# Gate and up projections of four feed-forward layers by seven block products in place of eight

## The chip, the core and the metric

One core of a Trainium2 chip runs the whole program. The metric is the device time of one execution in microseconds (us). The kernel before takes 2497.47 us (median of three runs, 2493.9 to 2501.86).

Engines are named as in the profile: PE (matrix products; PEld is its loading of the stationary operand), DVE (vector engine), ACT (activation engine), POOL (general engine), SP (a queue that issues transfers). Each engine works through its own list in order; semaphores tie the lists together.

## The reference

A sequence of 512 positions with 1024 features goes through four layers. Each adds a mixer's output to the stream and then a feed-forward block. Only this block matters here; it occurs four times (2816 hidden columns each):

```python
def swiglu(h, w_in, w_out):
    gu = h @ w_in
    gate, up = gu[..., :D_FF], gu[..., D_FF:]
    return (jax.nn.silu(gate) * up) @ w_out

x = x + swiglu(rmsnorm(x, norm_ffn_w[i]), ffn_w_in[i], ffn_w_out[i])
```

`rmsnorm` multiplies each position (a row of `h`) by one factor, 1/sqrt(mean of squares + eps), and each feature by a weight. Everything is float32.

## The kernel before

The stream lies transposed in eight tiles `xT[k]` of 128 features x 512 positions. Each float32 operand is split into a rounded part and a rest, `hi` and `lo`, both in the rounded type fp32r, and one product becomes three matmuls: hi*hi, hi*lo, lo*hi (`mm3`, L203 to L206).

**Weights.** `load_raw` (L173) fetches 512 KB (four 128-row tiles x 256 columns) into one of three buffers `wraw`. `split` (L166) makes `whi` on ACT (L169) and `wlo` on DVE, in some mixers on POOL (L164), 512 elements per partition at a time, two splits per transfer; there are seven `whi` and seven `wlo` buffers.

**Norm.** `norm` (L253) multiplies each `xT[k]` by the feature weight into `xh`, `xl` (L276, L277), squares on ACT, adds the squares on POOL (L269), and then makes the row factor: `xs.rc` (one column per 128 positions) and `xs.rb` (the same, broadcast over partitions). The row factor is applied to the products afterwards.

**Feed-forward.** `pair(jj)` (L356) works out 256 gate columns and 256 up columns: four output blocks of 128 x 512, each 8 feature tiles x 3 matmuls of 512 columns, so 96 matmuls; there are 11 pairs per layer. `evac` (L345) multiplies the gate block by the row factor (DVE L347), applies silu (ACT L349), multiplies by the row factor again (POOL L350) and by the up block (DVE L351), and splits the result into `hhi`, `hlo` (L220, L221). After pairs 0 to 3, 4 to 7 and 8 to 10 `out_part` (L369) multiplies by the output weights and adds into `xT` (L394); in the last layer `out_nat` (L395) does it in the layout of the output, with 128 x 512 blocks that end in square, row factor and store (L433 to L448).

**What sets the order.** The program text only says what depends on what. A list scheduler with a timeline model fixes the order of each engine's list when the program is built; buffers are handed out in rotation, and an instruction that writes a buffer waits until the previous user of it is done. The eight accumulation banks (128 x 512 float32) are shared in a feed-forward block as g 2, s 3, t 2, o 1 (`PB[4]`, L89).

Of the kernel before, what the change touches and what calls it, by code (L numbers as in the profile page):

```python
# [16 lines left out]
P = 128  # L17
# [40 lines left out]
def tile_net(ctx: ExitStack, tc: tile.TileContext, d, out, layers=(0, 1, 2, 3)):  # L58
# [33 lines left out]
    hidden = [None]  # L92
# [11 lines left out]
    WB = 7  # L104
# [61 lines left out]
    def split(raw, nk, n):  # L166
# [172 lines left out]
    def ffn(L, last=False, aside=None):  # L339
        wi, wd = f"in{L}", f"down{L}"  # L340
        xs = norm(f"ffn{L}")
        parts = [(0, 8), (8, 16), (16, 22)]
        hid = {}

        def evac(j, pg, pu):  # L345
            g = scr("fg")
            V.tensor_tensor(g, pg, xs.rb, op=ALU.mult)  # L347
            s = scr("fs")
            A.activation(s, g, AF.Silu)  # L349
            G.tensor_tensor(s, s, xs.rb, op=ALU.mult)  # L350
# [4 lines left out]

        def pair(jj):  # L356
            bg = load_a(wi, 0, KT, jj * 256, 256)
            bu = load_a(wi, 0, KT, DFF + jj * 256, 256)
            if jj == 0:
                pss = group_a(xs, [bg[0], bu[0], bg[1], bu[1]], ["g", "g", "s", "s"])  # L360
                evac(0, pss[0], pss[1])
                evac(1, pss[2], pss[3])
            else:
                for i in range(2):
                    pg = group_a(xs, [bg[i]], ["g"])[0]
                    pu = group_a(xs, [bu[i]], ["g"])[0]
                    evac(2 * jj + i, pg, pu)

        def out_part(p):  # L369
            a, b = parts[p]  # L370
# [5 lines left out]
            for g in range(4):  # L376
                blocks = load_a(wd, a, n, g * 256, 256)
                if p == 2 and g < 2:
# [8 lines left out]
                    for m, ps in enumerate(pss):  # L387
                        V.tensor_tensor(xT[m], ps, xT[m], op=ALU.add)
                    continue
                for i, b in enumerate(blocks):  # L390
# [3 lines left out]
                    V.tensor_tensor(xT[m], ps, xT[m], op=ALU.add)  # L394
# [1202 lines left out]
```

## Time and profile before

| | us |
|---|---|
| median of three runs | 2497.47 |
| profiled execution, its own time | 2493.01 |
| span of the profile | 2491.3 |
| PE busy | 2437.0 (98%) |
| DVE busy | 1419.6 (57%) |
| ACT busy | 998.0 (40%) |
| POOL busy | 526.7 (21%) |

The profiled execution's time is 1.7 us above its span. Busy time of PE is modelled: a matmul's shown duration runs past the start of the next one, so pace is read from the distance of starts, and idle time from the list of waits.

### The profile page before, as it was taken

The page shows a single profiled execution, that of the slowest core. Times are in us where ns is not written, and L with a number is a line of the kernel's source. Part 1 is how long each engine was busy: PE and PEld are TensorE (multiplying, and loading weights), DVE is VectorE, ACT ScalarE, POOL GpSimd, SP SyncE. Part 2 cuts the span into 40 slices and gives each one's busy share as a digit, 9 for nine tenths or more (in the row PEclk, how much of TensorE's full clock was granted, in tenths as well). Part 3 has the DMA queues.
Part 4 walks back from the last instruction along what each step waited for, and adds up shares of the span by engine and source line. Part 5 has one row for each costly group of instructions (what it writes and reads, how often), then busy time and mean ns, then how long its engine had stood idle before and what let it go on. Part 6 is the DMA issues. An engine that isn't in the chain of part 4 may idle for free. (4 is left out here: it accounts for less than half of the span.)

```text
span 2491.3 us, 30631 instructions
## 1 busy us (share of the span) xinstructions
PE 2437.0 (98%) x11316; PEld 1990.8 (80%) x11316; DVE 1419.6 (57%) x2613; ACT 998.0 (40%) x1900; POOL 526.7 (21%) x429
## 2 busy tenths in 40 slices
PE   8999999999999999999999988999999999999998
PEld 7897888888767888888767866888888888888887
DVE  6577644445786643435889978743434755434335
ACT  4444423334586432323554463432323323323333
POOL 3220101002362200101656345310101201100000
PEclk9999999999999999999999999999999999999999
DMA  4332333322311332332221133233332333223332
GB/s 138 115 100 69 94 102 94 100 91 89 106 39 35 93 101 94 100 95 86 73 78 60 52 108 96 92 95 101 93 101 78 110 102 102 94 89 104 96 96 74
DMA packets 73559, 226.26 MB, mean 91 GB/s; under 512 B 10353, under 2 KB 14593, under 8 KB 73409
## 3 DMA queue, kind: packets, MB, share of 16 engines
q1 hardware_dynamic: 68896, 220.00, 28.9%
q10 hardware_dynamic: 4464, 4.21, 0.6%
q8 instruction: 89, 1.46, 0.2%
q14 instruction: 62, 0.50, 0.1%
q0 software_dynamic: 48, 0.10, 0.0%
HBM read 219.45 MB, written 2.20 MB: 89 GB/s over the span
## 5 line engine op out<-in xcount | busy, mean ns | idle before, releaser
L169 ACT ACTIVATE whi<-wraw 128x512 fp32r<-128x512 f32 (+1 forms) x798 | 492.7, 622 | 1062.5 <-PE ps_g L205 702.8
L164 DVE TENSOR_TENSOR wlo<-wraw,whi 128x512 fp32r<-128x512 f32 (+1 forms) x738 | 540.8, 736 | 462.1 <-ACT whi L169 440.2
L204 PE MATMUL ps_g<-xh,whi 128*128 128x512 f32 x1976 | 780.8, 395 | 6.0 <-DVE fg L347 1.9
L205 PE MATMUL ps_g<-xl,whi 128*128 128x512 f32 x1976 | 776.1, 393 | 0.5 <-POOL xl L221 0.5
L206 PE MATMUL ps_g<-xh,wlo 128*128 128x512 f32 x1976 | 774.2, 392 | 0.0
L204 PEld LDWEIGHTS ps_g<-xh,whi 128*128 128x128 f32 x1976 | 372.9, 189 | 87.4 <-issue 4.3
L206 PEld LDWEIGHTS ps_g<-xh,wlo 128*128 128x128 f32 x1976 | 372.5, 188 | 79.3 <-issue 1.7
L205 PEld LDWEIGHTS ps_g<-xl,whi 128*128 128x128 f32 x1976 | 373.0, 189 | 77.6 <-issue 0.9
L350 POOL TENSOR_TENSOR fs<-fs,rb 128x512 f32<-128x512 f32 x88 | 114.5, 1302 | 1160.0 <-ACT fs L349 1160.0
L347 DVE TENSOR_TENSOR fg<-ps_g,rb 128x512 f32<-128x512 f32 x84 | 58.0, 691 | 142.9 <-PE ps_g L206 142.9
L351 DVE TENSOR_TENSOR fg<-ps_g,fs 128x512 f32<-128x512 f32 x84 | 58.0, 691 | 129.5 <-PE ps_g L206 128.0
L269 POOL TENSOR_TENSOR ssum<-ssum,sq 128x512 f32<-128x512 f32 x56 | 79.6, 1422 | 163.8 <-ACT sq L268 162.3
L164 POOL TENSOR_TENSOR wlo<-wraw,whi 128x512 fp32r<-128x512 f32 (+1 forms) x60 | 80.0, 1340 | 107.5 <-ACT whi L169 97.2
L204 PE MATMUL ps_s<-hhi,whi 128*128 128x512 f32 x264 | 102.7, 389 | 0.0
L205 PE MATMUL ps_s<-hlo,whi 128*128 128x512 f32 x264 | 102.7, 389 | 0.0
L206 PE MATMUL ps_s<-hhi,wlo 128*128 128x512 f32 x264 | 102.7, 389 | 0.0
L204 PE MATMUL ps_t<-hhi,whi 128*128 128x512 f32 x264 | 102.7, 389 | 0.0
L205 PE MATMUL ps_t<-hlo,whi 128*128 128x512 f32 x264 | 102.7, 389 | 0.0
L206 PE MATMUL ps_t<-hhi,wlo 128*128 128x512 f32 x264 | 102.7, 389 | 0.0
L220 ACT ACTIVATE hhi<-fg 128x512 fp32r<-128x512 f32 x88 | 55.6, 632 | 32.8 <-DVE fg L351 32.6
L277 DVE SCALAR_TENSOR_TENSOR xl<-xT,cols,xh 128x512 fp32r<-128x512 f32 x64 | 63.8, 1007 | 8.0 <-ACT xh L276 8.0
L349 ACT ACTIVATE fs<-fg 128x512 f32<-128x512 f32 x88 | 55.6, 632 | 30.8 <-DVE fg L347 30.8
(494 smaller groups left out, 3611.4 us busy)
## 6 DMA issues: line engine op xcount, KB each, us to landing
wraw<-in_in_dram SPq DMA_DIRECT2D x176, 512.0 KB, 3.5
wraw<-in_down_dram SPq DMA_DIRECT2D x82, 512.0 KB, 3.6
wraw<-in_par_in_dram SPq DMA_DIRECT2D x30, 512.0 KB, 3.5
wraw<-in_mlstm_in_dram SPq DMA_DIRECT2D x24, 512.0 KB, 4.0
wraw<-in_sc_in_dram SPq DMA_DIRECT2D x24, 512.0 KB, 3.7
wraw<-in_attn_in_dram SPq DMA_DIRECT2D x12, 512.0 KB, 3.8
wraw<-in_par_out_dram SPq DMA_DIRECT2D x12, 512.0 KB, 3.5
mb<-drs SPq DMA_DIRECT2D x16, 256.0 KB, 3.9
```

Of the source, the lines that this page charges most:

```text
L164: (V if e == "V" else G).tensor_tensor(lo, x, hi.bitcast(F32), op=ALU.subtract)
L169: A.activation(hi, raw, AF.Copy)
L204: T.matmul(o, lhsT=w[0], rhs=x[0], start=start, stop=False)
L205: T.matmul(o, lhsT=w[0], rhs=x[1], start=False, stop=False)
L206: T.matmul(o, lhsT=w[1], rhs=x[0], start=False, stop=stop)
L220: A.activation(hi, src, AF.Copy)
L269: G.tensor_tensor(ssum, ssum, sq, op=ALU.add)
L277: V.scalar_tensor_tensor(lo, xT[k], col(wname, k), hi.bitcast(F32), op0=ALU.mult, op1=ALU.subtract)
L347: V.tensor_tensor(g, pg, xs.rb, op=ALU.mult)
L349: A.activation(s, g, AF.Silu)
L350: G.tensor_tensor(s, s, xs.rb, op=ALU.mult)
L351: V.tensor_tensor(g, pu, s, op=ALU.mult)
```

## The change

The 1024 x 512 weight block of one pair (256 gate and 256 up columns) and the 1024 x 512 activations are each seen as a 2 x 2 matrix of blocks: weights by even and odd feature tile and by gate and up, activations by even and odd feature tile and by first and second half of the positions. The 2 x 2 product takes seven block products in place of eight, with sums of blocks ahead of and behind them (Winograd's form of Strassen's scheme).

- The four sums of activation blocks (`T1` to `T4`) are made once per layer (`combine`: two ACT scalings, three DVE subtractions, one split per pair of feature tiles).
- The weights of each pair are summed anew (`weights`): one addition on POOL (line 400 of the new kernel) and three subtractions on DVE (line 405), each 128 x 1024. Each of the seven operands is split 1024 wide (ACT line 170, DVE line 165).
- Each block product is 2 x 4 x 3 = 24 matmuls of 256 columns (lines 421 to 423) into one bank; products accumulate onto earlier ones in three of seven cases. ACT copies four intermediate sums out (`keep`, line 430), DVE adds them to later ones (lines 442, 448, 453, 455).
- Pair 0 of each layer is computed as before (96 matmuls of 512 columns), with banks s, o, s, o.
- The second row factor is taken off the hidden tile (the POOL multiplication is gone) and put on the output: `add_row` multiplies the output block by `xs.rb` (line 493) and then adds (line 494); in the last layer one instruction does both.
- Buffers: `wraw` five in place of three; `whi` and `wlo` four of 1024 in place of seven of 512, in the mixers too. The last layer's output runs in four parts (3, 3, 3, 2 pairs) in place of three. The rope tables use other buffers. The rows of the input weights are packed even tiles first.

```diff
-    WB = 7
+    WB = 4
+    RB = 5
...
-        return [(hi[:, k, :], lo[:, k, :]) for k in range(nk)]
+        return hi, lo
...
+            hi, lo = split(raw, m, n)
             for b in range(0, n, P):
-                res[b // P] += split(raw[:, :, b:b + P], m, P)
+                res[b // P] += [(hi[:, i, b:b + P], lo[:, i, b:b + P]) for i in range(m)]
...
-        parts = [(0, 8), (8, 16), (16, 22)]
+        parts = [(0, 3), (3, 6), (6, 9), (9, 11)] if last else [(0, 4), (4, 8), (8, 11)]
         hid = {}
...
+        rb2 = bass.AP(tensor=xs.rb.tensor, offset=xs.rb.offset, ap=[xs.rb.ap[0], [0, 2], [1, S]])
+        HS = slice(0, S // 2), slice(S // 2, S)
+        def gate(g):
+            V.tensor_tensor(g, g, rb2, op=ALU.mult)
+            A.activation(g, g, AF.Silu)
+        def store(jj, u):
+            n = 3 if last else 4
+            hi = hidden[0].tile([P, 2, S], F32R, tag="hhi", name="hhi", bufs=n)
+            lo = hidden[0].tile([P, 2, S], F32R, tag="hlo", name="hlo", bufs=n)
+            hilo(u, hi, lo)
+            for i in range(2):
+                hid[2 * jj + i] = (hi[:, i, :], lo[:, i, :])
+        tc_hi, tc_lo = [], []
+        def combine(i):
+            y = scr("S", (P, 2, S), bufs=3)
+            for h in range(2):
+                A.activation(y[:, h, :], xT[2 * i + h], AF.Copy, scale=col(f"ffn{L}", 2 * i + h))
+            t = scr("fu", (P, 4, S // 2))
+            hs = [y.ap[0], [S // 2, 2], [1, S // 2]]
+            V.tensor_tensor(t[:, 0:2, :], y[:, :, HS[1]], bass.AP(tensor=y.tensor, offset=y.offset, ap=hs),
+                            op=ALU.subtract)
+            V.tensor_tensor(t[:, 2, :], y[:, 1, HS[1]], t[:, 0, :], op=ALU.subtract)
+            V.tensor_tensor(t[:, 3, :], y[:, 1, HS[0]], t[:, 2, :], op=ALU.subtract)
+            hi = hidden[1].tile([P, 4, S // 2], F32R, tag="thi", name="thi", bufs=4)
+            lo = hidden[1].tile([P, 4, S // 2], F32R, tag="tlo", name="tlo", bufs=4)
+            hilo(t, hi, lo)
+            tc_hi.append(hi)
+            tc_lo.append(lo)
+        def quad(q):
+            if q[0] == "B":
+                k, h = int(q[1]) - 1, HS[int(q[2]) - 1]
+                return [(hi[:, h], lo[:, h]) for hi, lo in xs.t[k::2]]
+            n = ("T1", "T3", "T2", "T4").index(q)
+            return [(hi[:, n, :], lo[:, n, :]) for hi, lo in zip(tc_hi, tc_lo)]
+        STEPS = ("B11", "B21", "T1", "T2", "B22", "T3", "T4")
+        live = {}
+        def weights(jj, s):
+            if s == 0:
+                for n, (k, c) in enumerate(((0, 0), (4, 0), (0, DFF), (4, DFF))):
+                    live[jj, n] = load_raw(wi, k, c + jj * 256)
+                live[jj, "S1"] = scr("S", (P, 4, 256), bufs=3)
+                G.tensor_tensor(live[jj, "S1"], live[jj, 2], live[jj, 3], op=ALU.add)
+            r = [live[jj, n] for n in range(4)]
+            if s in (3, 4, 5):
+                t = scr("S", (P, 4, 256), bufs=3)
+                a, b = {3: (live[jj, "S1"], r[0]), 4: (r[1], live.get((jj, "S2"))), 5: (r[0], r[2])}[s]
+                V.tensor_tensor(t, a, b, op=ALU.subtract)
+                if s == 3:
+                    live[jj, "S2"] = t
             else:
...
+                t = {0: r[0], 1: r[1], 2: live[jj, "S1"], 6: r[3]}[s]
+            live[jj, "w", s] = split(t, 4, 256)
+        def product(jj, s, ps, start):
+            hi, lo = live.pop((jj, "w", s))
+            x = quad(STEPS[s])
+            for j in range(2):
+                o = ps[:, HS[j]]
+                for i in range(4):
+                    c = slice(j * P, (j + 1) * P)
+                    w = hi[:, i, c], lo[:, i, c]
+                    end = i == 3
+                    T.matmul(o, lhsT=w[0], rhs=x[i][0], start=start and i == j == 0, stop=False, skip_group_check=True)
+                    T.matmul(o, lhsT=w[0], rhs=x[i][1], start=False, stop=False, skip_group_check=True)
+                    T.matmul(o, lhsT=w[1], rhs=x[i][0], start=False, stop=end, skip_group_check=True)
+        def view(t):
+            return t.rearrange("p (j n) -> p j n", j=2)
+        def keep(ps):
+            t = scr("pc", bufs=4)
+            A.activation(t, ps, AF.Copy)
+            return view(t)
+        def seven(jj, ahead):
+            a, b, c, e = [bank(t) for t in "gsto"]
+            g, u = scr("fg", (P, 2, S)), None
+            for s, ps in enumerate((a, b, c, a, c, a, e)):
+                ahead()
+                product(jj, s, ps, s in (0, 1, 2, 6))
+                if s == 0:
+                    p1 = keep(a)
+                elif s == 1:
+                    V.tensor_tensor(g[:, :, HS[0]], view(b), p1, op=ALU.add)
+                elif s == 2:
+                    p5 = keep(c)
+                elif s == 3:
+                    u2 = keep(a)
+                elif s == 4:
+                    V.tensor_tensor(g[:, :, HS[1]], view(c), u2, op=ALU.add)
+                    gate(g)
+                elif s == 5:
+                    u3 = keep(a)
+                    u = scr("fu", (P, 2, S))
+                    V.tensor_tensor(u[:, :, HS[1]], view(a), p5, op=ALU.add)
+                else:
+                    V.tensor_tensor(u[:, :, HS[0]], view(e), u3, op=ALU.add)
+            V.tensor_tensor(u, u, g, op=ALU.mult)
+            store(jj, u)
+        ready = [0]
+        def run(jjs):
+            todo = [(jj, s) for jj in jjs for s in range(7)]
+            n = [0]
+            def ahead(lead=3):
+                while n[0] < min(len(todo), ready[0] + lead + 1):
+                    weights(*todo[n[0]])
+                    n[0] += 1
+                ready[0] += 1
+            ready[0] = 0
+            for jj in jjs:
+                seven(jj, ahead)
+        def first():
+            order = [0, 4, 1, 5, 2, 6, 3, 7]
+            bg = [[b[k] for k in order] for b in load_a(wi, 0, KT, 0, 256)]
+            bu = [[b[k] for k in order] for b in load_a(wi, 0, KT, DFF, 256)]
+            pss = group_a(xs, [bg[0], bu[0], bg[1], bu[1]], ["s", "o", "s", "o"])
+            for i in range(4):
+                combine(i)
+            g, u = scr("fg", (P, 2, S)), scr("fu", (P, 2, S))
+            for i in range(2):
+                V.tensor_tensor(g[:, i, :], pss[2 * i], xs.rb, op=ALU.mult)
+            A.activation(g, g, AF.Silu)
+            for i in range(2):
+                V.tensor_tensor(u[:, i, :], pss[2 * i + 1], g[:, i, :], op=ALU.mult)
+            store(0, u)
+        def add_row(m, ps):
+            t = scr("fg", (P, 2, S))[:, 0, :]
+            V.tensor_tensor(t, ps, xs.rb, op=ALU.mult)
+            V.tensor_tensor(xT[m], xT[m], t, op=ALU.add)
...
+                        add_row(m, ps)
                     continue
                 for i, b in enumerate(blocks):
                     m = 2 * g + i
                     ps = bank("sstt"[m % 4])
                     gemm(ps, b, kt)
-                    V.tensor_tensor(xT[m], ps, xT[m], op=ALU.add)
+                    add_row(m, ps)
...
-                        V.tensor_tensor(xnat[c][:, sl], pss[c], xnat[c][:, sl], op=ALU.add)
-                        if p == 2:
+                        V.scalar_tensor_tensor(xnat[c][:, sl], pss[c], xs.rc[:, c:c + 1], xnat[c][:, sl],
+                                               op0=ALU.mult, op1=ALU.add)
...
+        first()
+        for p, (a, b) in enumerate(parts):
+            run(range(max(a, 1), b))
+            if last:
+                if p == 0:
+                    xnat = to_nat()
+                elif p == len(parts) - 1:
+                    wfin = final_weight()
+            out_part(p)
+            if aside and p == 0:
+                aside()```

**DVE in the middle of a feed-forward block.** A row is one instruction (x2: two alike in a row) as it stands in the engine's list: line, operation, output<-inputs, shape. Before, one half of a pair:

```order
403 L347 TENSOR_TENSOR fg<-ps_g,rb 128x512
404 L164 TENSOR_TENSOR wlo<-wraw,whi 128x512 x2
405 L351 TENSOR_TENSOR fg<-ps_g,fs 128x512
406 L164 TENSOR_TENSOR wlo<-wraw,whi 128x512
407 L221 TENSOR_TENSOR hlo<-fg,hhi 128x512
408 L164 TENSOR_TENSOR wlo<-wraw,whi 128x512
```

And of the changed kernel most of a pair (`S` is a sum of weight blocks or its input, `pc` a copied-out sum, `fg` and `fu` the gate and up results):

```order
464 L165 TENSOR_TENSOR wlo<-wraw,whi 128x1024
465 L405 TENSOR_TENSOR S<-S,wraw 128x1024
466 L165 TENSOR_TENSOR wlo<-wraw,whi 128x1024
467 L405 TENSOR_TENSOR S<-wraw,S 128x1024
468 L448 TENSOR_TENSOR fg<-ps_t,pc 128x2x256
469 L165 TENSOR_TENSOR wlo<-wraw,whi 128x1024
470 L350 TENSOR_TENSOR fg<-fg,rb 128x1024
471 L165 TENSOR_TENSOR wlo<-S,whi 128x1024
472 L453 TENSOR_TENSOR fu<-ps_g,pc 128x2x256
473 L455 TENSOR_TENSOR fu<-ps_o,pc 128x2x256
474 L405 TENSOR_TENSOR S<-wraw 128x1024
475 L165 TENSOR_TENSOR wlo<-S,whi 128x1024
```

A pair has 14 DVE instructions of 512 before (two such halves); now it has 13 of 1024 and four of 512 (rows 464 to 480 are one round; the five after row 475 are L456, L165, L442, L165 and L223).

**DVE at the start of the first feed-forward block**, between the last tile of the norm and the row factor (`tlo` is the rest of an activation sum, `nv` the mean of squares). Before, with the rope tables (`rt`) that the scheduler drew into this place:

```order
356 L164 TENSOR_TENSOR wlo<-wraw,whi 128x512
357 L759 SCALAR_TENSOR_TENSOR rt<-rt 128x512
358 L164 TENSOR_TENSOR wlo<-wraw,whi 128x512
359 L759 SCALAR_TENSOR_TENSOR rt<-rt 128x512
360 L164 TENSOR_TENSOR wlo<-wraw,whi 128x512
361 L283 TENSOR_SCALAR nv<-ps_t 128x4
```

The same place in the changed kernel:

```order
330 L377 TENSOR_TENSOR fu<-S,fu 128x256
331 L376 TENSOR_TENSOR fu<-S,fu 128x256
332 L405 TENSOR_TENSOR S<-S,wraw 128x1024
333 L377 TENSOR_TENSOR fu<-S,fu 128x256
334 L223 TENSOR_TENSOR tlo<-fu,thi 128x1024
335 L405 TENSOR_TENSOR S<-wraw,S 128x1024
336 L223 TENSOR_TENSOR tlo<-fu,thi 128x1024
337 L165 TENSOR_TENSOR wlo<-wraw,whi 128x1024 x2
338 L285 TENSOR_SCALAR nv<-ps_t 128x4
```

The activation sums and the first weight sums of pair 1 now stand ahead of the splits for its first two products and ahead of the row factor; the rope tables have moved behind the first part of the layer.

**PE in the middle of a feed-forward block.** Of the changed kernel, where the fourth product (into `ps_g`) ends:

```order
1974 L422 MATMUL ps_g<-tlo,whi 128x256
1975 L423 MATMUL ps_g<-thi,wlo 128x256
1976 L421 MATMUL ps_o<-thi,whi 128x256
1977 L422 MATMUL ps_o<-tlo,whi 128x256
1978 L421 MATMUL ps_t<-xh,whi 128x256
1979 L422 MATMUL ps_t<-xl,whi 128x256
```

Two matmuls of the seventh product (`ps_o`) stand ahead of the fifth (`ps_t`), eight more behind it, and fourteen behind the sixth. Before, PE's list holds here the triples L204, L205, L206 of 128x512 one block after another.

## Rows read from the trace of the kernel before

**Rows 1.** The page: span, and busy time by engine.

```profile
span 2491.3 us, 30631 instructions
...
PE 2437.0 (98%) x11316; PEld 1990.8 (80%) x11316; DVE 1419.6 (57%) x2613; ACT 998.0 (40%) x1900; POOL 526.7 (21%) x429
```

**Rows 2.** Stretches: us, busy per engine, granted clock, DMA share, GB/s.

```profile
core 0: us, PE busy (x) PEld busy (x) DVE busy (x) ACT busy (x) POOL busy (x), PEclk, DMA share, GB/s
300.00:460.00 160.00, 160.00 (x708) 132.48 (x707) 65.16 (x99) 50.58 (x81) 14.23 (x11) 1.00 0.32 98
634.58:645.90 11.32, 11.32 (x97) 11.32 (x96) 6.24 (x7) 4.34 (x8) 5.13 (x3) 1.00 0.57 150
239.00:273.90 34.90, 31.54 (x144) 25.71 (x142) 34.48 (x59) 18.41 (x30) 9.67 (x7) 1.00 0.32 93
906.00:1176.00 270.00, 270.00 (x1193) 223.65 (x1192) 111.05 (x173) 84.64 (x138) 21.46 (x18) 1.00 0.30 92
2100.00:2140.00 40.00, 40.00 (x184) 33.27 (x183) 15.51 (x33) 13.02 (x22) 5.76 (x5) 1.00 0.25 79
```

**Rows 3.** PE's waits from 230 to 285 us: who, total, times, longest.

```profile
PE ps_g L204 <- DVE fg L347: 1.9, 1, 1.9
PE ps_g L204 <- ACT gk L220: 1.5, 1, 1.5
PE ps_s L204 <- DVE xT L323: 1.4, 1, 1.4
```

**Rows 4.** Timeline of PE, 512 columns: start, duration (fifteen rows, first and last).

```profile
335.94 0.39 PE L204 MATMUL ps_g<-xh,whi 128*128 128x512 f32 x1
...
339.11 0.39 PE L206 MATMUL ps_g<-xh,wlo 128*128 128x512 f32 x1
```

**Rows 5.** The same for 256 columns, in a mixer (47 rows, first and last).

```profile
56.40 0.28 PE L210 MATMUL ps_g<-whi,xh 128*128 128x256 f32 x1
...
61.92 0.28 PE L211 MATMUL ps_g<-whi,xl 128*128 128x256 f32 x1
```

**Rows 6.** Line L164: duration in ns min/median/max, first and last start, shapes.

```profile
L164 DVE TENSOR_TENSOR wlo<-wraw,whi x738: 411/685/1786, 20.2 to 2464.5; 128x512 fp32r<-128x512 f32 x173, 128x256 fp32r<-128x256 f32 x12
L164 POOL TENSOR_TENSOR wlo<-wraw,whi x60: 729/1291/2514, 13.5 to 1534.3; 128x512 fp32r<-128x512 f32 x56, 128x256 fp32r<-128x256 f32 x4
```

**Rows 7.** Timeline of DVE in the norm of the first feed-forward block.

```profile
248.27 0.68 DVE L323 TENSOR_TENSOR xT<-ps_s,xT 128x512 f32<-128x512 f32 x1
248.87 1.50 DVE L164 TENSOR_TENSOR wlo<-wraw,whi 128x512 fp32r<-128x512 f32 x1
...
255.35 0.68 DVE L164 TENSOR_TENSOR wlo<-wraw,whi 128x512 fp32r<-128x512 f32 x1
255.95 0.68 DVE L759 SCALAR_TENSOR_TENSOR rt<-rt 128x512 f32<-128x512 f32 x1
256.56 0.73 DVE L277 SCALAR_TENSOR_TENSOR xl<-xT,cols,xh 128x512 fp32r<-128x512 f32 x1
```

**Rows 8.** Timeline of POOL at the same place.

```profile
248.54 1.29 POOL L269 TENSOR_TENSOR ssum<-ssum,sq 128x512 f32<-128x512 f32 x1 [0.74 <-ACT sq L268]
```

**Rows 9.** Groups by shape: busy us, mean ns, idle before and releasers.

```profile
L347 DVE TENSOR_TENSOR fg<-ps_g,rb 128x512 f32<-128x512 f32 x84 | 58.0, 691 | 142.9 <-PE ps_g L206 142.9
...
L169 ACT ACTIVATE whi<-wraw 128x512 fp32r<-128x512 f32 x770 | 481.1, 630 | 1014.4 <-PE ps_g L205 683.8 <-PE ps_s L205 120.2 <-PE ps_t L205 111.4
```

**Rows 10.** DMA issues of the page: count, KB each, us to landing.

```profile
wraw<-in_in_dram SPq DMA_DIRECT2D x176, 512.0 KB, 3.5
```

**Rows 11.** Timeline of DVE at the end of the last layer.

```profile
2478.96 0.69 DVE L409 TENSOR_TENSOR xo<-ps_t,xo 128x512 f32<-128x512 f32 x1 [0.45 <-PE ps_t L212]
2479.76 0.75 DVE L446 SCALAR_TENSOR_TENSOR xo<-xo,fr,wfin 128x512 f32<-128x512 f32 x1
2480.50 0.16 DVE L439 SCALAR_TENSOR_TENSOR fmean<-fss,fmean 128x1 f32<-128x1 f32 x1
2483.04 0.69 DVE L409 TENSOR_TENSOR xo<-ps_t,xo 128x512 f32<-128x512 f32 x1 [0.45 <-PE ps_t L212]
2483.84 0.75 DVE L446 SCALAR_TENSOR_TENSOR xo<-xo,fr,wfin 128x512 f32<-128x512 f32 x1
```

More of the change, by code (lines that the diff above doesn't have):

```diff
@@ L90, in tile_net @@
     share(PB[4])
-    hidden = [None]
+    hidden = [None, None]
     def hid_tile(tag, bufs, dt=F32R):
@@ L195, in load_b @@
         res = []
-        mk, st = _W[w][3], 512 // n
+        mk = _W[w][3]
         for k in range(0, nk, mk):
             raw = load_raw(w, k0 + k, c0)
-            for i in range(0, mk, st):
-                res += split(raw[:, i:i + st, :], st, n)
+            hi, lo = split(raw, mk, n)
+            res += [(hi[:, i, :], lo[:, i, :]) for i in range(mk)]
         return res
@@ L377, in out_part @@
                 blocks = load_a(wd, a, n, g * 256, 256)
-                if p == 2 and g < 2:
+                if p == len(parts) - 1 and g < 2:
                     if g == 0:
@@ L393, in out_part @@
                     gemm(ps, b, kt)
-                    V.tensor_tensor(xT[m], ps, xT[m], op=ALU.add)
+                    add_row(m, ps)
         def out_nat(p, a, n, kt):
+            end = p == len(parts) - 1
             for half in range(2):
@@ L400, in out_nat @@
                 pss = [bank(t) for t in "sstt"]
-                if p == 2 and half == 1:
+                if end and half == 1:
                     order = [(c, k) for c in range(NCH) for k in range(n)]
@@ L448, in finish, with final_weight @@
                 nc.sync.dma_start(out[c * P:(c + 1) * P, halves[h]], x[:, halves[h]])
-        if last:
+        def final_weight():
             fw = d["final_norm_2"]
-            wfin = []
-            for h in range(2):
-                wfin.append(scr("wfin"))
-                nc.scalar.dma_start(wfin[h], bass.AP(tensor=fw.tensor, offset=fw.offset + h * 512, ap=[[0, P], [1, 512]]))
-        for jj in range(4):
-            pair(jj)
-            if last and jj == 0:
-                xnat = to_nat()
-        out_part(0)
-        if aside:
-            aside()
-        for jj in range(4, 8):
-            pair(jj)
-        out_part(1)
-        for jj in range(8, 11):
-            pair(jj)
-        out_part(2)
+            t = scr("fg", (P, 2, S))
+            nc.scalar.dma_start(t.rearrange("p h n -> p (h n)"),
+                                bass.AP(tensor=fw.tensor, offset=fw.offset, ap=[[0, P], [1, D]]))
+            return [t[:, h, :] for h in range(2)]
+        first()
[8 more added lines that the diff above has]
+            if aside and p == 0:
+                aside()
     def mlstm():
@@ L954, in parallel @@
             G.memset(raw[:, :, 72:96], 0.0)
-            sm += split(raw[:, :, 0:112], 4, 112)
+            hi, lo = split(raw[:, :, 0:112], 4, 112)
+            sm += [(hi[:, i, :], lo[:, i, :]) for i in range(4)]
         lay = ExitStack()
@@ L1508, in tile_net @@
         share(PB[4])
-        with tc.tile_pool(name=f"hf{L}", bufs=8) as hidden[0], tc.tile_pool(name=f"ff{L}", bufs=2) as phase[0]:
+        with tc.tile_pool(name=f"tf{L}", bufs=4) as hidden[1], tc.tile_pool(name=f"hf{L}", bufs=4) as hidden[0], \
+                tc.tile_pool(name=f"ff{L}", bufs=2) as phase[0]:
             ffn(L, last=last, aside=rope_tables if before_window else None)
```

42 lines of the change are left out of this document (12 added, 30 removed).

## Prediction

> **What bounds the kernel now.** I read the page first: PE is busy 2437 of 2491.3 us, DVE 57%, ACT 40%, POOL 21% [rows 1]. A share says nothing about a stage, so the table of stretches comes next. Inside feed-forward blocks PE is busy 160.00 of 160 us and 270.00 of 270 us at a granted clock of 1.00, with DVE at 65.16 of 160 us (41%) [rows 2]. The list of PE's waits confirms it: around the start of the first block there are three short ones, 4.8 us together, of which the one on L347 and the one on xT (3.3 us) lie inside the block [rows 3]; the stretch over a later block has none [rows 2]. So only fewer or cheaper matmuls shorten these blocks, until another engine needs as long as PE. The reader is to see two questions: what 256 columns cost against 512, and how much DVE has left.
>
> **Removed on PE.** A pair has 96 matmuls of 512 columns. Fifteen starts in a row lie 3.17 us apart over 14 steps, 0.2264 us each [rows 4] (the stretch gives 160/708 = 0.226 [rows 2]), so a pair takes 96 x 0.2264 = 21.73 us. The seven products have 7 x 24 = 168 matmuls of 256 columns. Such matmuls exist in the mixers, with a fresh stationary tile for each one, as here: 47 starts, 5.52 us over 46 steps, 0.1200 us [rows 5]; a second stretch shows 11.32/97 = 0.117 [rows 2]. 168 x 0.1200 = 20.16 us. One eighth of the work would be 2.72 us; the halves cost more than half (0.1200 against 0.1132), and 1.57 us is left. Ten of eleven pairs in four layers: 40 x 1.57 = 63 us. The other matmuls keep their number.
>
> The Trainium skill, "TensorE: Matmul & The Clock Gate", section "Back-to-back issue gap", gives N/2.4 + 2.5 ns for matmuls one behind the other, so 109 ns for 256 columns; a pair would then be 18.4 us and the gain twice as large. The row of this case has 120 ns, and the row decides.
>
> **Added on DVE, per pair.** A 1024-wide instruction is not in the trace. A 512-wide one starts 0.60 us after the one before it when both are ready (255.35 to 255.95) [rows 7]; medians and minimum of 512 and 256 columns (685 and 411 ns) differ by 1.07 ns per element [rows 6], so 1024 take 0.60 + 512 x 0.00107 = 1.15 us. Ends: 1.10 (the slope alone) and 1.37 (twice 0.685). I take 1.15, since the rows show the fixed part being paid once per instruction. One round has 13 of these (seven splits, three weight sums, row factor, product, rest of the hidden tile) and four of 512 that read a bank, which also start 0.60 us apart (248.27 to 248.87 [rows 7]; 691 ns shown [rows 9]): 13 x 1.15 + 4 x 0.60 = 17.35 us.
>
> POOL's sum of 1024 is bounded by its 512-wide subtraction: 1.29 us, slope (1291 - 729)/256 = 2.2 ns, so 1.29 + 1.12 = 2.41 us [rows 6]. It costs DVE too. Where POOL adds from 248.54 to 249.83 [rows 8], a DVE subtraction of two on-chip operands that started at 248.87 takes 1.50 us instead of 0.68 and ends 0.54 us after POOL's end [rows 7]: DVE stood still. In the worst case all 2.41 us are lost: 17.35 + 2.41 = 19.76 us of 20.16, 98%. DVE goes from 41% busy to nearly full; the forecast hangs on the remaining 0.4 us.
>
> Is the order kind to it? I walk one round, with PE's pair from 0 and products 2.88 us apart. L455 waits for the end of the pair before and is done at 1.9 in the settled round (why, below); L405, L165, L456, L165 reach 6.5; L442 7.1 (its product ended at 5.76); L165 and L223 9.4; the split for the seventh product 10.6, or 13.0 with POOL's sum inside; L405, L165, L405 16.4; L448 17.0 (fifth product ended at 14.64); L165, L350 19.3. The next L165 needs a buffer that the sixth product frees at 18.48, and ACT's 1.26 us (two of 630 ns [rows 9]) before it, so it starts at 19.7 and ends at 20.9; L453 and L455 end at 22.1, which is 1.9 in the next round. That repeats and doesn't drift. Against it PE's needs: the seventh product's rest is needed at 14.64 and is there at 13.0, margin 1.6 us; the others have 4 us or more. So PE does not wait in a settled round, but the smallest margin is 1.6 us. I charge 0.2 us per pair for late transfers and first rounds after an output part: 8 us. Ends: 0 and, with 1.37 us per instruction, 13 x 0.22 = 2.9 us more DVE (a rival below).
>
> Other engines beside it: ACT has nine instructions of 1024 and four of 512, at most 9 x 1.26 + 4 x 0.63 = 13.9 of 20.16 us [rows 9]. Transfers stay at four of 512 KB per pair, 3.5 us to landing [rows 10]; five buffers replace three, but four are held until the fourth to seventh split, so three of the next pair's four transfers are issued in the first 3 us of a round and land well ahead of the walk's 10.6.
>
> **Start of a block.** `combine` adds on DVE four times 0.60 + 2 x 0.33 + 1.15 = 2.41 us, 9.7 us, and the splits and sums of pair 1 come earlier. In the first block DVE was already full, 34.48 of 34.90 us, and PE stood 3.3 us [rows 2, 3]; the rope tables leave this place, so it stays about as it was. The last block's start had DVE busy 15.51 of 40 us [rows 2]; with 9.7, three weight sums (3.5), three more splits (3.5) and POOL's eight sums of squares holding it for part of 10 us it comes to about 35 to 40. The order puts the splits for pair 1's first two products behind all of that, and PE has 72 matmuls (16.3 us) in front of them, since one of four blocks must wait for bank o. I take 2 us more per block, 8 us; ends 0 and 20.
>
> **Small terms.** `add_row` puts one more DVE instruction behind the last output block of three layers: 3 x 0.6 = 2 us; elsewhere it lies beside the 192 matmuls of a part (192 x 0.2264 = 43 us). In the last part of the last layer a chunk has 12 matmuls (2.7 us) in place of 18 (4.08 us between the two L409 [rows 11]), while its DVE chain, 3.3 us from L439 to L446 plus a wait on the evacuation, stays; three chunks lose up to 1 us each: 3 us. Wider splits and deeper weight buffers in the mixers: 0, between -8 and +8, since a first split lands about 1 us later and transfers start earlier. POOL's L350 (two per half pair) goes; nothing waited on it.
>
> Sum on the profiled execution's own 2493.0 us: -63 + 8 + 8 + 2 + 3 = -42, so 2451. That execution was 4.5 us below the median of the runs; on the median's scale 2455 us.
>
> **Rivals.**
> - *DVE a little over PE.* The sum on POOL and the splits on DVE hold each other up, and in-order waits on banks add to a nearly full engine. With two 512-pieces of 0.60 per instruction, 13 x 1.21 + 2.4 + 2.41 = 20.5, plus 0.5 us of waits: 21.0 per pair. Gain 40 x 0.73 = 29, less 13: 2477, on the median's scale 2481. For it: 41% to 98% leaves no room, and L405 depends on POOL. Against it: the walk closes. The Trainium skill, "SBUF — State Buffer", section "Who interferes with whom", says that whichever of the two starts first holds the port for its whole instruction; by that rule POOL's sum can also be put off behind DVE's 1.15 us, which the walk leaves out.
> - *Slower: DVE bound.* If a 1024-wide instruction costs twice the shown 0.685 us, DVE needs 13 x 1.37 + 4 x 0.69 + 2.41 = 23.0 us per pair, 1.25 over the old 21.73: +50 + 13, so 2556, on the median's scale 2560. It decides from 1.27 us per instruction on, where DVE's round passes 21.73. Against it: starts 0.60 apart [rows 7].
> - *No gain on PE.* If the 256-column pace in this place is 0.129 us or more (half banks alternate, products accumulate onto older sums), the pair is as long as before: about 2500 to 2510. Against it: two stretches at 0.120 and below.
> - *All hidden.* The starts and rounds cost nothing and the mixers gain from five buffers: 2493 - 63 + 4.5 = 2434.
>
> **Numbers.** Forecast 0.55 (its own range 2440 to 2470), DVE a little over 0.20, all hidden 0.10, DVE bound 0.10, no gain on PE 0.05. A change below 0.3%, 7.5 us, can't be told from none: faster means below 2490. Faster: the first three less 0.02 that the second ends above 2490, 0.83; slower: DVE bound and a part of the fifth, 0.12; same: 0.05. Range 2433 to 2490: it reaches from the all-hidden case over the forecast and the second case and leaves out some 0.17.
>
> **What would show it.** In the changed kernel's trace: starts of 256-column matmuls 0.120 us apart and a pair in 20.2 to 20.6 us; PE's waits in the blocks under 20 us in all, most at block starts on L165; DVE above 90% in the gate stretches; L165 at about 1.2 us, longer where L400 runs. Wrong: PE waiting on L165 or L405 in every pair, L165 at 1.3 us or more, or the 256-column starts farther apart.

## Result and profile after

The changed kernel takes 2512.39 us (median of ten runs, 2504.3 to 2515.35); the kernel before, beside it, 2497.51 (2493.9 to 2503.25). Ratio 1.0053, 95% interval 1.0041 to 1.0066: slower by half a per cent, where 2455 was forecast. The profiled execution took 2504.3 us, at the low end of its runs, so the spans differ by 10.9 us where the medians differ by 14.9.

The page of the changed kernel, against [rows 1]:

```profile
span 2502.2 us, 35838 instructions
...
PE 2391.4 (96%) x14196; PEld 2087.2 (83%) x14196; DVE 1865.7 (75%) x2664; ACT 1139.0 (46%) x1739; POOL 526.8 (21%) x350
```

PE is busy 46 us less, and the span is longer: idle PE time (span less busy) has doubled, from 54 to 111 us. The stretches say where. The columns are those of [rows 2]:

```profile
394.00:475.00 81.00, 81.00 (x675) 80.92 (x674) 69.79 (x65) 44.08 (x51) 8.26 (x3) 1.00 0.33 107
255.00:310.00 55.00, 46.89 (x273) 42.66 (x272) 44.93 (x56) 27.46 (x34) 17.45 (x8) 0.88 0.20 60
1200.00:1245.00 45.00, 31.19 (x137) 24.86 (x136) 33.49 (x49) 17.52 (x24) 27.20 (x18) 0.81 0.21 70
1960.00:1980.00 20.00, 15.43 (x60) 12.35 (x59) 9.78 (x23) 2.97 (x5) 2.62 (x2) 0.74 0.13 42
```

The first row is the four pairs of one output part: PE never idle, DVE 86% busy over the whole part. The others are a block's start, the start of the parallel mixer and that of the short convolution: PE stands, and the granted clock is below full.

To add it up I cut both traces at the start of the last addition of a mixer into `xT` (DVE) and at the start of the last matmul that reads `hhi` (PE); the tail is what follows the last of these. Times in us, layer by layer:

| | mixer 0 | block 0 | mixer 1 | block 1 | mixer 2 | block 2 | mixer 3 | block 3 | tail |
|---|---|---|---|---|---|---|---|---|---|
| before | 254.8 | 356.4 | 220.1 | 356.7 | 400.7 | 354.2 | 175.9 | 363.8 | 8.7 |
| after | 258.8 | 352.6 | 223.9 | 351.3 | 417.2 | 350.0 | 189.6 | 349.1 | 9.7 |

Ten pairs at 1.57 us less should shorten each block by 15.7. They became 3.8, 5.4, 4.2 and 14.7 us shorter, 28 together, so 35 us of the 63 are lost inside the blocks, nearly all in the first three. The mixers lose 4.0, 3.8, 16.5 and 13.7, together 38, and the tail 1: -63 + 35 + 38 + 1 = +11.

Idle PE time is most of what is lost. Summed over the four blocks, of the changed kernel and of the kernel before:

```profile
sum 1402.91, PE 1378.42 PEld 1280.00 DVE 1082.79 ACT 626.55 POOL 156.50; mean PE 344.60 PEld 320.00 DVE 270.70 ACT 156.64 POOL 39.13
sum 1431.15, PE 1428.57 PEld 1182.40 DVE 642.26 ACT 480.20 POOL 147.88; mean PE 357.14 PEld 295.60 DVE 160.56 ACT 120.05 POOL 36.97
```

That is 24.5 us idle for 2.6, so 22 of the 35; in the mixers, cut the same way, it is 77.0 for 43.4, 34 of the 38. The rest is time in which PE worked more slowly: the mean granted clock is 0.98, 0.99 and 0.99 in the first three blocks, 1.00 before.

**Inside a pair nothing is lost.** PE's timeline in the first block (start, duration; nine rows, first and last):

```profile
395.81 0.28 PE L421 MATMUL ps_g<-xh,whi 128*128 128x256 f32 x1
...
396.77 0.28 PE L423 MATMUL ps_g<-xh,wlo 128*128 128x256 f32 x1
```

0.96 us over eight steps is 0.120 us, as in [rows 5], and four pairs take 81 us, 20.2 each. DVE is nearly full there: two rounds in a row, each with all 17 instructions (columns of [rows 2]), and one subtraction that POOL's sum L400 held up:

```profile
414.10:434.23 20.13, 20.13 (x170) 20.13 (x170) 19.46 (x17) 10.31 (x13) 2.40 (x1) 1.00 0.32 109
434.23:454.39 20.16, 20.16 (x171) 20.16 (x170) 18.98 (x17) 11.14 (x14) 3.45 (x1) 1.00 0.32 101
444.56 2.87 DVE L165 TENSOR_TENSOR wlo<-wraw,whi 128x1024 fp32r<-128x1024 f32 x1 [0.49 <-ACT whi L170]
```

**The start of a block.** PE's waits over the whole first block:

```profile
PE ps_g L421 <- ACT whi L170: 8.1, 1, 8.1
```

There is one, before the first of the seven products; the second block has the same of 8.1 us; the third has six short ones, 7.5 us together. The releaser is ACT's split. ACT's list ahead of it (the bracket is the idle time before the row and what ended it):

```profile
266.98 0.63 ACT L270 ACTIVATE sq<-xT 128x512 f32<-128x512 f32 x1 [4.63 <-POOL ssum L271]
271.64 1.06 ACT L222 ACTIVATE thi<-fu 128x1024 fp32r<-128x1024 f32 x1 [4.03 <-DVE fu L377]
272.60 0.62 ACT L270 ACTIVATE sq<-xT 128x512 f32<-128x512 f32 x1
273.44 1.06 ACT L222 ACTIVATE thi<-fu 128x1024 fp32r<-128x1024 f32 x1 [0.23 <-DVE fu L377]
277.97 0.63 ACT L270 ACTIVATE sq<-xT 128x512 f32<-128x512 f32 x1 [3.47 <-POOL ssum L271]
278.50 1.99 ACT L170 ACTIVATE whi<-wraw 128x1024 fp32r<-128x1024 f32 x2
```

And POOL's, at the same place:

```profile
262.00 3.25 POOL L400 TENSOR_TENSOR S<-wraw 128x1024 f32<-128x1024 f32 x1 [1.55 <-DVE wlo L165]
...
273.29 4.64 POOL L271 TENSOR_TENSOR ssum<-ssum,sq 128x512 f32<-128x512 f32 x1 [4.05 <-ACT sq L270]
```

DVE beside that last addition:

```profile
273.33 1.21 DVE L223 TENSOR_TENSOR tlo<-fu,thi 128x1024 fp32r<-128x1024 f32 x1
274.47 1.21 DVE L405 TENSOR_TENSOR S<-wraw,S 128x1024 f32<-128x1024 f32 x1
275.60 1.21 DVE L223 TENSOR_TENSOR tlo<-fu,thi 128x1024 fp32r<-128x1024 f32 x1
```

These are read together. The norm's squares go one by one from ACT through a single `sq` buffer to POOL. The combinations (L222, L377) and the first sum of weights (L400) now stand among them in the three lists. ACT's last square but one (272.60) stands behind a combination's split, which waits for DVE; POOL's addition of it (1.29 us in [rows 8]) takes 4.64 us beside a busy DVE; the last square (277.97) waits for that addition, and the split that PE needs is behind the last square. Then the clock: PE had stood 8.1 us, and its next matmuls come at the lower level (1.2 GHz):

```profile
282.11 0.41 PE L421 MATMUL ps_g<-xh,whi 128*128 128x256 f32 x1
...
285.31 0.41 PE L421 MATMUL ps_g<-xh,whi 128*128 128x256 f32 x1
```

Fifteen steps of 0.213 us in place of 0.120; the slow starts go on to 287.9. From 280.2 on that is 7.7 us at 0.56 of the pace, by estimate 3.4 us lost on top of the stall. Over the whole span the mean granted clock fell:

```profile
core 0: 2502.2 us, clock 0.979
```

Before it was 0.993. At two levels, 1.0 and 0.5, that is 2 x 0.021 x 2502 = 105 us at half level against 2 x 0.007 x 2491 = 35.

**The parallel mixer.** PE's longest wait in the changed kernel is here (the two of L245 between 1180 and 1260 us):

```profile
PE ps_t L245 <- DVE nrc L295: 9.5, 1, 9.5
...
PE ps_t L245 <- DVE nrc L234: 2.0, 1, 2.0
```

`nrc` is the second row factor of this norm (a final norm stands ahead of it), a chain of short DVE instructions. DVE:

```profile
1226.35 0.16 DVE L234 SCALAR_TENSOR_TENSOR nrc<-rs_z,nrc 128x4 f32<-128x4 f32 x1
1226.55 1.13 DVE L232 TENSOR_TENSOR rs_z<-nrc 128x4 f32<-128x4 f32 x1
...
1233.81 1.19 DVE L295 TENSOR_TENSOR nrc<-nrc 128x4 f32<-128x4 f32 x1
```

POOL at the same time:

```profile
1226.40 9.80 POOL L1414 TENSOR_TENSOR xT<-xT,rb 128x512 f32<-128x512 f32 x8 [3.41 <-ACT rb L246]
```

From the moment at which POOL multiplies eight tiles by the first row (1.2 us each), each short DVE instruction takes 1.13 to 1.19 us in place of 0.16: one per POOL instruction. The Trainium skill, "SBUF — State Buffer", section "Who interferes with whom", says that a DVE instruction with two on-chip inputs and a POOL instruction that reads there shut each other out; these rows agree for seven of the eight DVE instructions. The eighth (L1363, at 1235.03) has one input and takes 1.19 us as well. Before, the same chain stood ahead of the multiplications (DVE, DVE, POOL):

```profile
1216.45 0.16 DVE L232 SCALAR_TENSOR_TENSOR nrc<-rs_z,nrc 128x4 f32<-128x4 f32 x1
1216.64 0.16 DVE L293 TENSOR_TENSOR nrc<-nrc 128x4 f32<-128x4 f32 x1
1222.35 13.05 POOL L1286 TENSOR_TENSOR xT<-xT,rb 128x512 f32<-128x512 f32 x8
```

**The short convolution.** Before, PE had not one wait between 1943 and 1966 us. Now, between 1954 and 1980:

```profile
PE ps_t L245 <- DVE nrc L234: 2.4, 1, 2.4
PE ps_g L206 <- DVE ct L1601: 2.1, 1, 2.1
```

PE turns to the row factor 14.5 us after the block's last product starts, before 14.7, so it was always about that late; before, PE worked into another bank meanwhile (`ps_s`, from 1952.4 on). Now its list has no product into `ps_s` before 1981.8, and ACT has no weight split between 1957.6 and 1976.7; that split then waits for a buffer that PE's `ps_g` products free:

```profile
1976.71 1.06 ACT L170 ACTIVATE whi<-wraw 128x1024 fp32r<-128x1024 f32 x1 [6.60 <-PE ps_g L207]
```

One thing is later than before: the norm's last input. The last addition into `xT` ends 7.9 us after the block's last product starts, 4.0 before; `add_row` is in it, and other DVE work ahead of it. ACT waits for it:

```profile
1961.81 0.73 ACT L278 ACTIVATE xh<-xT,cols 128x512 fp32r<-128x512 f32 x1 [3.69 <-DVE xT L494]
```

### The profile page after: what moved, and what is told of

It reads as the page before. It is cut to its first block, busy times and chain, and to the rows that moved or that the text cites. A ratio compares the mean times of both kernels' runs of the same rounds, so it can differ in the third digit from the quotient of the medians.

```text
span 2502.2 us, 35838 instructions
## 1 busy us (share of the span) xinstructions
PE 2391.4 (96%) x14196; PEld 2087.2 (83%) x14196; DVE 1865.7 (75%) x2664; ACT 1139.0 (46%) x1739; POOL 526.8 (21%) x350
## 4 chain that ended last, share of the span: by engine, by line
PE 83%; DVE 9%; ACT 3%; DMA 2%; issue 2%; POOL 1%; ACTq 0%; SPq 0%; DVEq 0%; POOLq 0%
PE ps_g L206 6%; PE ps_g L207 6%; PE ps_g L208 6%; PE ps_g L423 5%; PE ps_g L421 5%; PE ps_g L422 5%; PE ps_s L206 3%; PE ps_s L207 3%; PE ps_s L208 3%; PE ps_t L423 3%; PE ps_t L422 3%; PE ps_t L421 3%; PE ps_t L206 3%; PE ps_t L207 3%; PE ps_t L208 3%
## 5 line engine op out<-in xcount | busy, mean ns | idle before, releaser
L170 ACT ACTIVATE whi<-wraw 128x1024 fp32r<-128x1024 f32 x358 | 372.9, 1044 | 544.3 <-PE ps_g L207 150.8
L165 DVE TENSOR_TENSOR wlo<-wraw,whi 128x1024 fp32r<-128x1024 f32 (+1 forms) x329 | 428.5, 1306 | 186.9 <-ACT whi L170 186.0
L400 POOL TENSOR_TENSOR S<-wraw 128x1024 f32<-128x1024 f32 x40 | 110.0, 2749 | 1012.9 <-DMA wraw<-in_in_dram 949.4
L170 ACT ACTIVATE whi<-S 128x1024 fp32r<-128x1024 f32 x160 | 169.5, 1060 | 244.5 <-PE ps_g L422 110.3
L206 PE MATMUL ps_g<-xh,whi 128*128 128x512 f32 (+1 forms) x632 | 258.2, 409 | 9.2 <-DVE ucv L1602 2.3
L165 DVE TENSOR_TENSOR wlo<-S,whi 128x1024 fp32r<-128x1024 f32 x160 | 210.9, 1319 | 64.4 <-ACT whi L170 64.2
L207 PE MATMUL ps_g<-xl,whi 128*128 128x512 f32 (+1 forms) x632 | 254.3, 403 | 0.2 <-DVE xl L279 0.2
L208 PE MATMUL ps_g<-xh,wlo 128*128 128x512 f32 (+1 forms) x632 | 253.7, 402 | 0.0
L423 PE MATMUL ps_g<-thi,wlo 128*128 128x256 f32 x640 | 181.4, 283 | 0.3 <-DVE wlo L165 0.3
L422 PE MATMUL ps_g<-tlo,whi 128*128 128x256 f32 x640 | 181.3, 283 | 0.0
L421 PE MATMUL ps_g<-thi,whi 128*128 128x256 f32 x640 | 181.3, 283 | 0.0
L206 PEld LDWEIGHTS ps_g<-xh,whi 128*128 128x128 f32 (+1 forms) x632 | 120.9, 191 | 39.5 <-issue 5.3
L207 PEld LDWEIGHTS ps_g<-xl,whi 128*128 128x128 f32 (+1 forms) x632 | 121.2, 192 | 26.1 <-issue 2.0
L271 POOL TENSOR_TENSOR ssum<-ssum,sq 128x512 f32<-128x512 f32 x56 | 92.5, 1651 | 236.8 <-ACT sq L270 236.8
L423 PEld LDWEIGHTS ps_g<-thi,wlo 128*128 128x128 f32 x640 | 122.9, 192 | 0.5 <-DVE wlo L165 0.5
L421 PEld LDWEIGHTS ps_g<-thi,whi 128*128 128x128 f32 x640 | 123.0, 192 | 0.1
L422 PEld LDWEIGHTS ps_g<-tlo,whi 128*128 128x128 f32 x640 | 122.9, 192 | 0.1
L421 PE MATMUL ps_g<-xh,whi 128*128 128x256 f32 x320 | 94.1, 294 | 17.7 <-ACT whi L170 17.7
L207 PE MATMUL ps_s<-hlo,whi 128*128 128x512 f32 x264 | 102.9, 390 | 0.0
L206 PE MATMUL ps_t<-hhi,whi 128*128 128x512 f32 x264 | 102.8, 389 | 0.0
## 6 DMA issues: line engine op xcount, KB each, us to landing
wraw<-in_in_dram SPq DMA_DIRECT2D x176, 512.0 KB, 3.6
wraw<-in_down_dram SPq DMA_DIRECT2D x82, 512.0 KB, 3.6
wraw<-in_par_in_dram SPq DMA_DIRECT2D x30, 512.0 KB, 3.5
wraw<-in_mlstm_in_dram SPq DMA_DIRECT2D x24, 512.0 KB, 3.8
wraw<-in_sc_in_dram SPq DMA_DIRECT2D x24, 512.0 KB, 3.5
wraw<-in_attn_in_dram SPq DMA_DIRECT2D x12, 512.0 KB, 4.1
wraw<-in_par_out_dram SPq DMA_DIRECT2D x12, 512.0 KB, 3.6
```

The source lines that it names most:

```text
L165: (V if e == "V" else G).tensor_tensor(lo, x, hi.bitcast(F32), op=ALU.subtract)
L170: A.activation(hi, raw, AF.Copy)
L206: T.matmul(o, lhsT=w[0], rhs=x[0], start=start, stop=False)
L207: T.matmul(o, lhsT=w[0], rhs=x[1], start=False, stop=False)
L208: T.matmul(o, lhsT=w[1], rhs=x[0], start=False, stop=stop)
L271: G.tensor_tensor(ssum, ssum, sq, op=ALU.add)
```

## Experiments

Theories: **W**, the mixers lose by the 1024-wide splits; **S**, a block loses at its start by what stands there; the letters of later theories are explained in their expectations. Each result is a median beside the kernel before on the same chip (2496.7 to 2496.9).

**1. Only the weight handling.** The kernel before, with

```diff
-    WB = 7
+    WB = 4
-                res[b // P] += split(raw[:, :, b:b + P], m, P)
+            hi, lo = split(raw, m, n)
```

and, as in the changed kernel, five raw buffers and `dynamic_dma_scratch_size=4096`. Expected: 

> The kernel before (plain pairs everywhere) with only the change's weight handling: splits 1024 wide, four of them, five raw buffers. Theory W, that the wider splits slow the mixers: their stretches grow as in the changed kernel, +38 us by the two traces (+4 mlstm, +4 window, +17 parallel, +14 short_conv), so about 2535. Rival B, that the mixers lose only by what stands in the lists around the ends and starts of the seven-product blocks: 2497 within 5.

Measured: 2514.4, ratio 1.0063 (1.0042 to 1.0084). Half of what W expected by the median; the profiled execution, at the high end, has a span of 2518.4. Cut as above, the mixers lose 13.8, 4.5, -0.8 and 8.3: the window about as in the changed kernel (3.8), the short convolution less (13.7 there), mixer 0 more than three times as much (4.0 there), the parallel mixer nothing. So the weight handling as a whole costs, and the parallel mixer's loss is something else.

**2. Narrow splits in the changed kernel.**

```diff
-    WB = 4
+    WB = 8
-            live[jj, "w", s] = split(t, 4, 256)
+            live[jj, "w", s] = [split(t[:, :, b:b + P], 4, P) for b in (0, P)]
```

and the 128-column and 512-wide pieces of before in `load_a`, `load_b`. Expected: 

> The changed kernel with every split 512 wide again (eight buffers of half the size, the seven products too). Theory W: the mixers get back most of their 38 us, the pairs pay DVE 7 x 0.07 us = 0.5 each, which stands just at their PE time (20.2 against 20.16): 2475 to 2490. Rival B: 2512 to 2530.

Measured: 2479.95, ratio 0.9921 (0.9895 to 0.9946). This one edit turns slower into faster, by 32 us; the profiled executions are 22 apart, 15 in the mixers and 7 in the blocks. Mixer 0 is back at 254.3 and the short convolution at 178.3 us (189.6 with wide splits). The first 31 us behind block 2, of the changed kernel and of this run (columns of [rows 2]):

```profile
1953.90:1984.90 31.00, 26.43 (x108) 21.49 (x107) 18.01 (x30) 8.69 (x11) 6.00 (x5) 0.83 0.25 82
1944.50:1975.50 31.00, 28.87 (x134) 23.85 (x133) 23.07 (x41) 9.74 (x17) 5.44 (x4) 1.00 0.31 102
```

PE stands 2.1 us in place of 4.6, the clock stays full, and products into `ps_s` stand ahead of the row factor again (from 1954.7). W holds there; the window mixer gains nothing (227.5 us for 223.9), and the parallel mixer keeps 14 us of its loss. The start of block 0 keeps its stall, which PE's waits now show at the column sums:

```profile
PE ps_t L241 <- POOL ssum L273: 10.5, 1, 10.5
```

POOL's timeline has the instruction that it waits for:

```profile
269.08 7.66 POOL L273 TENSOR_TENSOR ssum<-ssum,sq 128x512 f32<-128x512 f32 x1 [4.04 <-ACT sq L272]
```

This addition of the norm takes 7.66 us: DVE works without a gap from 269.12 to 275.6, and it ends 1.1 us after that.

**3. Two plain pairs at a block's start** (changed kernel, wide):

```diff
         first()
+        second()
-            run(range(max(a, 1), b))
+            run(range(max(a, 2), b))
```

(`second`, not shown, computes pair 1 as `first` computes pair 0.) Expected: 

> The changed kernel with the first two pairs of a block plain, so that the combinations of x and the first sum of weights have 22 us more. Theory S, that a block loses its 10 to 12 us at its start because they stand ahead of the first seven products in the lists: the 8.1 us stalls at the starts go, 4 x 10 us come back and 4 x 1.57 are paid: about 2478. Rival, that the start is only late by what the mixer's end left (a late norm): the stalls stay or move into the second pair: 2512 to 2520.

Measured: 2501.0, ratio 1.0010 (0.9999 to 1.0022): 11 us back, a third of what S expected. The wait is only moved: PE stands 3.1 us in block 0 for ACT's split of the second pair, still behind the squares and combinations.

**4. The first sum of weights on DVE** (changed kernel, wide):

```diff
-                G.tensor_tensor(live[jj, "S1"], live[jj, 2], live[jj, 3], op=ALU.add)
+                (V if jj == 1 else G).tensor_tensor(live[jj, "S1"], live[jj, 2], live[jj, 3], op=ALU.add)
```

Expected: 

> The changed kernel with the sum of the first seven-product pair of a block (one instruction of 3.3 us on POOL among the squares of the norm) on DVE. Theory P, that this instruction holds the squares and through the one sq buffer ACT: 5 us or more back in each of the first three starts, 2490 to 2498. Theory C, that the combinations' own work on DVE and ACT is what is late: DVE gets 1.1 us more, 2512 to 2516.

Measured: 2505.9, ratio 1.0030 (1.0019 to 1.0041). Between the two: 6 us back, and a stall of 7.7 us at block 0 stays. POOL's sum is a small part of it.

**5. The combinations behind the norm** (with narrow splits):

```diff
+        cw = scr("cw", (P, KT), bufs=1)
+        V.scalar_tensor_tensor(cw, xs.rc[:, 0:1].to_broadcast([P, KT]), 0.0, col8(f"ffn{L}"),
+                               op0=ALU.mult, op1=ALU.add)
-    A.activation(y[:, h, :], xT[2 * i + h], AF.Copy, scale=col(f"ffn{L}", 2 * i + h))
+    A.activation(y[:, h, :], xT[2 * i + h], AF.Copy, scale=cw[:, 2 * i + h:2 * i + h + 1])
```

Expected: 

> The changed kernel with 512-wide splits and the combinations made to read their column scales through one small DVE instruction that reads the norm's result, so that no instruction of them can stand among the squares of the norm. Theory N, that the starts are late because ACT's next square waits in its list behind a combination that waits for DVE, and POOL's addition then finds DVE busy (one took 7.66 us): the stalls of 10.5 and 4.3 us at the column sums go, 5 to 8 us for each block with what the clock gives back: 2450 to 2460. Theory C, that it is the amount of the combinations' work: the wait moves to the third product of pair 1, 2475 to 2485.

Measured: 2492.56, ratio 0.9982 (0.9971 to 0.9993), 13 us slower than run 2. The wait at the column sums is gone and another stands at the products that read the combinations:

```profile
PE ps_t L429 <- ACT whi L174: 4.8, 1, 4.8
PE ps_g L431 <- DVE wlo L169: 1.6, 1, 1.6
```

Theory N alone falls: ahead of the row factor the combinations hold the norm, behind it they are late themselves.

**6. Both 3 and 5** (narrow splits). Expected: 

> As the run before, with the second pair of a block plain too. Theory N: nothing more is to be had, and 4 x 1.57 us are paid: 2456 to 2466. Theory C: the work now has 22 us more beside it: under 2465, and 10 us or more below the run before.

Measured: 2452.13, ratio 0.9819 (0.9802 to 0.9836). 40 us less than run 5 for one more plain pair. Block 0 takes 342.6 us, and 356.4 - 9 x 1.57 = 342.3: the start costs nothing more. Amount and place both matter.

**7. Second row first** (narrow splits):

```diff
-            xs.rb1 = bcast_rows(rcs[0], row_tile())
+            rb1 = row_tile()
         xs.rb = bcast_rows(xs.rc, row_tile())
+        if pre:
+            xs.rb1 = bcast_rows(rcs[0], rb1)
```

Expected: 

> The changed kernel with 512-wide splits and, in the norm that has a final norm ahead of it (the parallel mixer's), the second row broadcast before the first, so that POOL's eight multiplications of x by the first row can't run beside the short DVE instructions of the second rsqrt. Theory L, that those multiplications hold the short instructions (0.16 us each before, 1.19 us in the changed kernel): the 9.0 us wait of PE goes, 6 to 12 us back with the clock: 2468 to 2474. Rival, that the second row is late for the splits ahead of it on DVE: 2478 to 2484.

Measured: 2467.11, ratio 0.9878 (0.9861 to 0.9894), 13 us less than run 2; the parallel mixer takes 406.9 us for 414.6, and PE's wait is 4.2 (9.0 in run 2, the second line):

```profile
PE ps_t L247 <- DVE nrc L297: 4.2, 1, 4.2
PE ps_t L247 <- DVE nrc L297: 9.0, 1, 9.0
```

L holds, for 7.7 us of the parallel mixer's loss; run 9 against run 6 shows the same, 408.2 for 416.2. About half of that loss is left. The other difference from run 2 is not the edit's: PE's list is the same in both up to the parallel mixer, and the profiled executions are 12.7 us apart by there. In one PE waits 10.5 us for POOL's held addition in block 0, in the other 4.1; the window mixer takes 227.5 and 222.0 us with PE idle 11.6 and 12.6, at a mean granted clock of 0.94 and 0.98. So a stage cut out of one execution is good to some 5 us.

**8. No combinations** (narrow splits): `combine` is not called, and `quad` returns halves of `xs.t`, so the kernel leaves the four activation sums out and its products are not the block's; only its time counts. Expected: 

> The changed kernel with 512-wide splits and without the combinations of x (the products T1 to T4 read halves of x as it is, so the combinations are left out of the computation). Prices them in full, work and place together. Theory N and theory C both: 7 to 12 us for each block, 2435 to 2455; a rival, that the starts are late through the mixers' ends alone: 2475 to 2482.

Measured: 2448.96, ratio 0.9805 (0.978 to 0.9829). 31 us for the combinations; in the profiled executions 26 to 27 of them lie in the blocks. Blocks 0 and 1 take 341.4 us each, which is 356.4 - 15.7 and 0.7 more.

**9. All together**, runs 6 and 7 in one. Expected: 

> All three together: 512-wide splits, two plain pairs at a block's start with the combinations behind the norm's result, second row broadcast first. If the three causes are separate their gains add: 2452 less the 13 us of the row's order, 2437 to 2445. If the row's order only moved a wait that the other two also remove: 2450 to 2455.

Measured: 2442.8, ratio 0.9786 (0.9773 to 0.9799): 54 us faster than before, 70 than the change as it was. Block 0's start, the stretch of the table above:

```profile
255.00:310.00 55.00, 54.96 (x322) 48.49 (x321) 47.71 (x74) 33.25 (x49) 6.04 (x3) 1.00 0.25 81
```

PE works through at full clock, with 9 pairs in place of 10 by seven products.

**10. The same without the edit of run 5.** Expected: 

> The same without the instruction that holds the combinations behind the norm. Theory N (their place among the squares matters also where they have the time of two pairs): 10 us or more slower than the kernel beside it, 2450 to 2460. Theory C (only their amount beside one pair): within 4 us of it.

Measured: 2456.93, ratio 0.9841 (0.9827 to 0.9855): 14 us slower than run 9. With the time of two pairs, the place still decides.

**11. The kernel before with the edit of run 7.** Expected: 

> The kernel before with the second row broadcast first and nothing else. In its trace the second rsqrt runs through in 0.16 us steps ahead of POOL's multiplications, so if the long wait in the changed kernel is of the changed kernel's order, this gives nothing: 2493 to 2500. If it is a fault that both have: 2485 to 2490.

Measured: 2499.64, ratio 1.0014 (1.0005 to 1.0023): no gain. The long wait belongs to the order that the changed kernel's lists came out in.

## Why the prediction was wrong

- *A pair on PE: 20.16 us.* Right: 0.120 us per start, 20.2 us per pair, and no rival at the pair came.
- *DVE per pair: 17.35 us, 19.76 with POOL's sum.* Right: full rounds have 18.98 and 19.46 us, what POOL held up included, 94 and 97% of the pair; no pair lost by it. "DVE above 90%" came so. My mark for wrong, L165 at 1.3 us, was reached and meant nothing: the page's mean is 1.31 with the waits for POOL in it (1.22 alone, 2.87 beside L400 in the row above). The 8 us charged for rounds were not needed.
- *Start of a block: +2 each, 8 in all, ends 0 and 20.* **The first step that failed.** It cost 35 us: 11.9, 10.3, 11.5 and 1.0. PE's waits in the first two blocks are one each, at the start, and not on L165. I added up DVE's work and set it against 16.3 us of PE's matmuls; I had the order in view, but did not follow the chain of squares through it, where ACT, POOL and DVE hand one buffer round. Run 8 gives the price of the combinations (31 us), run 5 that moving them alone doesn't help, runs 6 and 10 that time and place together do.
- *Wider splits in the mixers: 0, -8 to +8.* **The second.** The mixers lost 38 us. Runs 1 and 2 put the width among the causes. I had reasoned "a first split lands 1 us later". At the short convolution it is whether PE has products into another bank to turn to while the row factor is late. The reading that four large buffers are held together while eight small ones come free one by one fits ACT's wait there; no run shows it by itself. By the cuts, the sum of the mixers is 38 us above before in the changed kernel, 23 in run 2, 7 in run 7 and 8 in run 9.
- *Within the mixers, the parallel one* lost 16.5 us, about 8 of them by a thing that no term held: the scheduler's new order let POOL's multiplications run beside the short chain of DVE (runs 7, 9 and 11). The other half is open.
- *The clock had no term.* After the 8.1 us stall PE came back at 1.2 GHz, and the stretches of the parallel mixer and the short convolution show a mean clock of 0.81 and 0.74; block 0's start lost some 3.4 us so behind 8.1 of waiting. Over the four blocks 13 of the 35 us are not idle time. A stall is to be priced with that.
- *Tail +3, `add_row` +2.* The tail came to +1, and the last block, where the other chunks lie, lost 1.0 in all. `add_row` shows in no wait of PE, but in one of ACT: 3.7 us for `xT` at the short convolution. No run takes it alone, so its price, in part inside the mixers' 38, is open.
- *Two slips in the working* change no term: 168 x 0.109 us is 18.3 and not 18.4, and L350 ran once per half pair, not twice.

The sum was forecast as -63 + 8 + 8 + 2 + 3 + 0 = -42 and came out as -63 + 35 + 38 + 1 = +11. The slower rival that I wrote, DVE bound in every pair, was not the one that came. Left open: the last 7 to 8 us in the mixers of runs 7 and 9, most of them in the parallel mixer, and what each stall costs through the clock alone; no run separates it.

## What to carry to other kernels

A change that spares work on the bounding engine is settled where that engine is bound; look for its price in the stages at both sides, where other engines set the pace. For an added preparation, follow each in-order list from the last input to the first user, buffer by buffer: a chain that hops between three engines through one buffer is held by whatever a scheduler puts between. Coarser instructions can cost more than their latency (run 2: 32 us for halving the splits at the same buffer space); that they free buffers in larger lumps is the likely reason.

## What the runs showed of the hardware

- One POOL addition that takes 1.29 us in [rows 8] took 4.64 and 7.66 us beside DVE instructions in a row without a gap: it was held over several of them and ended 1.1 us after the last.
- The other way round, eight DVE instructions of 0.16 to 0.17 us took 1.13 to 1.19 each, one per POOL multiplication.
- At the lower clock level 256-column matmuls start 0.213 us apart, 1.78 times 0.120 and not twice.
